# Four of eleven pairs of SwiGLU column blocks by seven products of quarters

## The chip, the cores and the metric

The kernel runs on one core of one Trainium2 chip. A core has a matrix engine (TensorE, PE in the profile; its weight loads are the row PEld), VectorE (DVE), ScalarE (ACT), GpSimd (POOL) and SyncE (SP), which run side by side and wait for each other by semaphores. Loads from device memory are issued here by SP, stores and a few small loads by POOL; an issuing engine takes its DMAs in order, and one that has to wait holds up those behind it. The metric is the device time of one launch in microseconds; lower is better.

## The reference

Two layers over 512 tokens of 1024 features, in float32. Each layer is a SwiGLU half step, a token mixer, and a second SwiGLU half step, with a layer norm after each:

```python
def swiglu(x, w13, w2):
    a, b = jnp.split(x @ w13, 2, axis=-1)
    return (jax.nn.silu(a) * b) @ w2
...
for l in range(DEPTH):
    x = layer_norm(ALPHA * x + 0.5 * swiglu(x, ffn1_w13[l], ffn1_w2[l]), ln_g[l, 0], ln_b[l, 0])
    m = mixer(x, w_in[l], ...)
    x = layer_norm(ALPHA * x + m, ln_g[l, 1], ln_b[l, 1])
    x = layer_norm(ALPHA * x + 0.5 * swiglu(x, ffn2_w13[l], ffn2_w2[l]), ln_g[l, 2], ln_b[l, 2])
```

`w13` is 1024 x 5632 (a and b of 2816 columns each), `w2` is 2816 x 1024. There are four SwiGLUs in all. The mixer is not touched by the change, except for when the transposes behind its last projection fall due.

## The kernel before

**Arithmetic.** Every float32 operand is split into a high part (ScalarE copies it to the rounded type that PE takes, line 118) and the rest (VectorE subtracts, line 119). A product is three matmuls: high times high, high times low, low times high. The features of x lie transposed in four pairs of tiles, `xh` and `xl`.

**First products of a SwiGLU (`ffn`, from line 444).** The 2816 columns of a and of b are 22 blocks of 128 columns. Block j takes a weight block of a and one of b (512 KB each, tiles `r_a`, `r_b`, loaded by SP into 4 buffers; their split parts lie in 10 buffers of the tag `w`). `proj` runs 24 matmuls 128x512 into a bank `pa` and 24 into `pb`. `glu` takes SiLU of `pa` on ScalarE and multiplies by `pb` on VectorE (line 463) into the tile `r` of the pair of blocks k and k+11. So there are eleven pairs, made in the order 8, 9, 10, 0, 1, ..., 7, with 96 matmuls each. The first pair of a SwiGLU that follows another stage runs in halves of 256 tokens, since the tokens' features come in halves.

**Sums for the second products.** The product with `w2` is done by seven products of quarters in place of eight (Winograd's form of Strassen's scheme); class `Seven` prepares and runs it. When a pair of blocks is done, `activation_sums(k)` makes four sums and two splits of `r` on VectorE and ScalarE, and `weight_sums(k)` (lines 278 to 290) loads the pair's `w2` in two tiles `ra_w` and `rb_w` (512 KB each, SP), makes four sums on VectorE, three of them in place, and POOL stores each to device memory, from where `run` loads them. `ra_w` and `rb_w` come from a tag `rs` that has two buffers in all: the next pair's loads wait until the stores of this pair's sums have been read out of them.

**Second products (`run`, lines 331 to 442).** For k = 0 to 10 it loads weights and sums, splits them and runs 18 matmuls 128x512 for each k in a first phase (products P1, P6 and P5 of two token tiles each), then two more phases. P6 of k = 2 and 3 takes the tile `t22`, that of k = 0 and 1 `t20`. `later(k)` splits the two remaining sums of `r`. `norm` does the layer norm of a token tile, stores it, and puts its transposes (`to_features`) on a list of side work (`Flow`), due 11.5 us of counted matmul time later.

**Order.** A scheduler fixes each engine's order when the program is built, by its own estimate of when each instruction could run. At run time an engine takes its instructions strictly in that order, and a VectorE instruction that waits holds up all behind it. Eight banks hold PE's results, so four blocks are in flight.

Of the kernel before, what the change touches and what calls it, by code (L numbers as in the profile page):

```python
# [79 lines left out]
def trunk(ctx: ExitStack, tc, x_in, xt_in, w13, w2, w_in, w_br, w_out, ln_g, ln_b, lb_in, hgn, sgg, sgb, sgws,  # L83
# [12 lines left out]
    def bank(name):  # L96
        return psum.tile([P, 512], F32, tag="ps", name=name)
# [89 lines left out]
    def norm(t, xt, sums, g, b, last):  # L187


        nm = small("nm")  # L190
        V.tensor_scalar(nm, sums[:, 0:1], sums[:, 1:2], -1.0 / D, op0=ALU.add, op1=ALU.mult)
        sq = wk.tile([P, D], F32, tag="rs", name="sq", bufs=2)
        ssq = small("ssq")
        S.activation(sq, xt, AF.Square, bias=nm, accum_out=ssq)
        rstd = rstd_of(ssq, 1, 1.0 / D, LN_EPS / ALPHA ** 2, "rstd")
        for qs in H:
            V.scalar_tensor_tensor(xt[:, qs], xt[:, qs], nm, g[:, qs], op0=ALU.add, op1=ALU.mult)
            V.scalar_tensor_tensor(xt[:, qs], xt[:, qs], rstd, b[:, qs], op0=ALU.mult, op1=ALU.add)
            if last:
                nc.sync.dma_start(out[0, t * P:(t + 1) * P, qs], xt[:, qs])  # L200
        if not last:
            x_at[t] = dram.tile([P, D], F32, name=f"xd{t}", tag=f"xd{t}", bufs=2)
            nc.gpsimd.dma_start(x_at[t], xt)
            ready[t] = flow.add(to_features(t, xt), LN_NS)

    LN_NS = 11500.0
    ready = [None] * NT

    def need(*ts):
        for t in ts:  # L210
            if ready[t] is not None:
                flow.finish(ready[t])
                ready[t] = None

    def out_proj(nk, lhs, w_of, c, ln, tag):

        ys = [[bank(f"y{t}{q}") for q in range(2)] for t in range(NT)]
        w = {}
# [12 lines left out]
        for k in range(nk):  # L231
            w[k] = weights(w_of(k), f"{tag}{k}")
            if k < nk - tail:
                for t in range(NT):
                    unit(k, t, (0, 1))
        g, b = ln_params(*ln)
        xs = load_rows()
        begin_features()
        for t in range(NT):
            sums = small("sums", 2)  # L240
            for q in range(2):
                for k in range(nk - tail, nk):
                    unit(k, t, (q,))
                add_to(xs[t], q, c, ys[t][q], sums)
            norm(t, xs[t], sums, g, b, False)

    def load_rows():
        xs = []
# [10 lines left out]
    class Seven:  # L259
# [11 lines left out]

        def part(self, k, a):

            if k not in self.r:
                self.r[k] = quads(f"r{k}")
            return self.r[k][:, a::2, :]

        def weight_sums(self, k):
            w = self.w_of(k)
# [51 lines left out]
        def run(self, c, ln, last):  # L331
# [103 lines left out]
            for tt in range(2):  # L435
# [5 lines left out]
                add_to(xs[t], 0, c, F[tt], sums[t])  # L441
                norm(t, xs[t], sums[t], g, b, last)

    def ffn(l, i, last=False, first_of_all=False):
        made = list(range(Seven.KEPT, NH2)) + list(range(Seven.KEPT))
        seven = Seven(lambda k: w2[l, i, k])
        js = [j for k in made for j in (k, k + NH2)]

        def blocks(j, early=False):
            return (weights(w13[l, i, j], f"a{j}", early), weights(w13[l, i, NF + j], f"b{j}", early),  # L450
                    bank(f"pa{j}"), bank(f"pb{j}"))

        def pair_of(j, args, n0, n):
            wa, wb, pa, pb = args
            proj(pa, wa, 0, from_x, KT, n0, n)
            proj(pb, wb, 0, from_x, KT, n0, n)

        def glu(j, args):
            wa, wb, pa, pb = args
            k, a = j % NH2, j // NH2  # L460
            sa = wk.tile([P, T], F32, tag="sa", name="sa", bufs=NSA)
            S.activation(sa, pa, AF.Silu)
            V.tensor_tensor(seven.part(k, a), sa.rearrange("p (h t) -> p h t", h=2),  # L463
                            pb.rearrange("p (h t) -> p h t", h=2), op=ALU.mult)
            if a:
                seven.activation_sums(k)
                seven.weight_sums(k)

        start = 0 if first_of_all else 2
        first = [blocks(j, True) for j in js[:start]]  # L470
        need(0, 1)
        for z, j in enumerate(js[:start]):
            pair_of(j, first[z], 0, 256)
        need(2, 3)
        for z, j in enumerate(js[:start]):
            pair_of(j, first[z], 256, 256)
            glu(j, first[z])
        for z, j in enumerate(js[start:]):
            if z == 0 and first_of_all:
                begin_features()  # L480
                wa = load_wx(w13[l, i, j])
                for q in range(1, 4):
                    load_xt(q)
                wb = weights(w13[l, i, NF + j], "b0")
                args = wa, wb, bank("pa0"), bank("pb0")
            else:
                args = blocks(j)
            pair_of(j, args, 0, T)
            glu(j, args)
        seven.run(0.5 / ALPHA, (l, 2 * i), last)  # L490

    def gates():
# [478 lines left out]
```

## Time and profile before

| | |
|---|---|
| time, median of 3 runs | 2124.06 us (2122.80 to 2125.29) |
| the profiled execution's own time | 2122.98 us |
| its span in the trace | 2120.1 us (2.9 us lie around it) |
| PE busy | 2097.9 us, 99% of the span, 10024 matmuls |
| VectorE busy | 1226.6 us, 58% |
| ScalarE busy | 772.2 us, 36% |
| GpSimd busy | 214.6 us, 10% |
| mean granted clock of PE | 0.998 |
| moved by DMA | 381 MB, 180 GB/s on average |

Busy time counts an engine's instructions; matmuls overlap, so what one matmul costs is read from the distance between starts, not from its own length. The chain of work is the profile's path back from the last instruction to what released it. A timeline row gives start, length, engine, line, operation, tiles, and in brackets the idle time ahead of it with what ended it. The waits list who waited for whom. A row of a DMA gives size and median time from issue to landing. Line numbers are those of the kernel before.

### The profile page before, as it was taken

To read this page: it belongs to the slowest core of one execution; us is meant where nothing else is said; L and a number is where in the kernel's file an instruction comes from. 1 tells how busy PE (TensorE), PEld (TensorE's weight loads), DVE (VectorE), ACT (ScalarE), POOL (GpSimd) and SP (SyncE) were. 2 spreads that over 40 slices of the span, in tenths; PEclk is the share of its full clock that TensorE was granted. 3 is DMA by queue.
4 is the path that set the end of the run, shared out by engine and by line. 5 is a ranking of instruction groups with operands and counts; after the bars stand their busy time and mean duration, and the time that the engine had idled before them with its cause. 6 is when DMAs were issued, how large, how long until landed. Compare 5 with 4: busy or idle time off the path is not lost.

```text
span 2120.1 us, 26533 instructions
## 1 busy us (share of the span) xinstructions
PE 2097.9 (99%) x10024; PEld 1761.5 (83%) x10024; DVE 1226.6 (58%) x2019; ACT 772.2 (36%) x1090; POOL 214.6 (10%) x360
## 2 busy tenths in 40 slices
PE   8999999999999999999999999999999999999998
PEld 6888888888888888888898888888888888888886
DVE  5545578843535644548754456779344456454586
ACT  4222455224322422226522234552333324222363
POOL 0101002001000110101111010020010001110101
PEclk9999999999999999999999999999999999999999
DMA  7665777122242465557757557761222426655674
GB/s 268 215 209 179 251 254 263 42 80 80 82 157 90 162 235 185 192 207 275 249 186 235 179 203 237 273 227 42 89 89 89 141 90 202 211 192 201 224 262 143
DMA packets 113905, 381.01 MB, mean 180 GB/s; under 512 B 14321, under 2 KB 14577, under 8 KB 113777
## 3 DMA queue, kind: packets, MB, share of 16 engines
q1 hardware_dynamic: 88848, 291.68, 42.0%
q0 software_dynamic: 24928, 87.64, 10.9%
q8 instruction: 78, 1.28, 0.2%
q14 instruction: 51, 0.41, 0.1%
HBM read 311.11 MB, written 68.16 MB: 179 GB/s over the span
## 4 chain that ended last, share of the span: by engine, by line
PE 80%; DVE 2%; ACT 1%; DMA 1%; POOL 0%; issue 0%; POOLq 0%; DVEq 0%; ACTq 0%
PE pa L143 17%; PE pb L143 16%; PE z L143 8%; PE pA L341 4%; PE pC L341 4%; PE y L143 4%; PE y L226 3%; PE pF L341 2%; PE q L143 2%; PE pE L341 2%; PE f L143 2%; PE pB L341 2%; PE i L551 2%; PE g L143 2%; PE v L551 2%; PE u L143 2%
## 5 line engine op out<-in xcount | busy, mean ns | idle before, releaser
L143 PE MATMUL pa<-xh,h_a 128*128 128x512 f32 (+1 forms) x752 | 285.0, 379 | 11.2 <-ACT xh L118 11.0
L143 PE MATMUL pa<-xl,h_a 128*128 128x512 f32 (+1 forms) x752 | 284.6, 378 | 0.1
L143 PE MATMUL pa<-xh,l_a 128*128 128x512 f32 (+1 forms) x752 | 283.7, 377 | 0.0
L143 PE MATMUL pb<-xh,h_b 128*128 128x512 f32 (+1 forms) x752 | 283.1, 377 | 0.0
L143 PE MATMUL pb<-xh,l_b 128*128 128x512 f32 (+1 forms) x752 | 282.4, 376 | 0.3 <-DVE l_b L119 0.3
L143 PE MATMUL pb<-xl,h_b 128*128 128x512 f32 (+1 forms) x752 | 282.4, 375 | 0.0
L119 DVE TENSOR_TENSOR l_b<-r_b,h_b 128x1024 fp32r<-128x1024 f32 x132 | 161.5, 1224 | 166.4 <-ACT h_b L118 165.8
L118 ACT ACTIVATE h_b<-r_b 128x1024 fp32r<-128x1024 f32 x132 | 139.9, 1060 | 303.6 <-PE pa L143 245.4
L463 DVE TENSOR_TENSOR r<-sa,pb 128x512 f32<-128x512 f32 x88 | 60.5, 688 | 303.3 <-PE pb L143 303.3
L118 ACT ACTIVATE h_a<-r_a 128x1024 fp32r<-128x1024 f32 (+1 forms) x89 | 93.5, 1051 | 278.9 <-PE pb L143 264.2
L143 PEld LDWEIGHTS pa<-xh,h_a 128*128 128x128 f32 x752 | 142.9, 190 | 38.4 <-ACT xh L118 12.6
L143 PEld LDWEIGHTS pa<-xl,h_a 128*128 128x128 f32 x752 | 142.2, 189 | 28.0 <-DVE xl L119 2.3
L143 PEld LDWEIGHTS pa<-xh,l_a 128*128 128x128 f32 x752 | 142.4, 189 | 25.6
L143 PEld LDWEIGHTS pb<-xl,h_b 128*128 128x128 f32 x752 | 141.7, 188 | 25.8
L143 PEld LDWEIGHTS pb<-xh,l_b 128*128 128x128 f32 x752 | 141.6, 188 | 26.1 <-DVE l_b L119 0.8
L143 PEld LDWEIGHTS pb<-xh,h_b 128*128 128x128 f32 x752 | 141.7, 188 | 25.5
L119 DVE TENSOR_TENSOR l_a<-r_a,h_a 128x1024 fp32r<-128x1024 f32 (+1 forms) x89 | 107.7, 1210 | 16.2 <-ACT h_a L118 12.3
L143 PE MATMUL z<-xh,h_z 128*128 128x512 f32 x256 | 102.6, 401 | 0.0
L285 POOL DMA_DIRECT2D t<-t x44 | 23.9, 543 | 763.8 <-DVE t L284 697.5
L143 PE MATMUL z<-xh,l_z 128*128 128x512 f32 x256 | 99.8, 390 | 0.0
L143 PE MATMUL z<-xl,h_z 128*128 128x512 f32 x256 | 99.8, 390 | 0.0
L119 DVE TENSOR_TENSOR l_z<-r_z,h_z 128x1024 fp32r<-128x1024 f32 x32 | 39.2, 1225 | 72.5 <-ACT h_z L118 72.4
(270 smaller groups left out, 4246.5 us busy)
## 6 DMA issues: line engine op xcount, KB each, us to landing
r_b<-in_w_dram SPq DMA_DIRECT2D x88, 512.0 KB, 4.7
r_a<-in_w_dram SPq DMA_DIRECT2D x87, 512.0 KB, 4.7
ra_w<-in_w_dram SPq DMA_DIRECT2D x44, 512.0 KB, 5.5
rb_w<-in_w_dram SPq DMA_DIRECT2D x44, 512.0 KB, 5.2
t<-ra_w POOLq DMA_DIRECT2D x88, 256.0 KB, 2.6
r_c<-in_w_dram SPq DMA_DIRECT2D x44, 512.0 KB, 6.3
r_d<-t SPq DMA_DIRECT2D x44, 512.0 KB, 4.6
r_z<-in_w_in_dram SPq DMA_DIRECT2D x32, 512.0 KB, 3.5
```

Of the source, the lines that this page charges most:

```text
L118: S.activation(hi, src, AF.Copy)
L119: V.tensor_tensor(lo, src, hi.bitcast(F32), op=ALU.subtract)
L143: PE.matmul(ps[:, n0:n0 + n], a[:, cs], m[:, n0:n0 + n], start=(i == 0), stop=(i == 3 * nk - 1))
L226: PE.matmul(ys[t][q], a[:, ts], m[:, q * 512:(q + 1) * 512], start=(k == 0 and i == 0), stop=(k == nk - 1 and i == 2))
L285: nc.gpsimd.dma_start(self.t1[k], t1)
L341: PE.matmul(ps[tt], a[:, ts], m, start=(start and k == 0 and z == 0), stop=(stop and k == NH2 - 1 and z == 2), skip_group_check=not start)
L463: V.tensor_tensor(seven.part(k, a), sa.rearrange("p (h t) -> p h t", h=2), pb.rearrange("p (h t) -> p h t", h=2), op=ALU.mult)
L551: PE.matmul(pss[t], a[k // 2][:, k % 2, ts], m[:, cs], start=(k == 0 and i == 0), stop=(k == KT - 1 and i == 2))
```

## The change

Of the eleven pairs of blocks, pairs 0 to 3 of each SwiGLU are now made by `seven_pair`: the 1024 input features and the 512 tokens are halved, a and b are the two column halves, and seven products of quarters take the place of eight. A product is 24 matmuls 128x256 for the pair's two blocks, so a pair is 168 matmuls 128x256 in place of 96 of 128x512. The sums that the scheme needs are made on VectorE: those of x once per SwiGLU (`x_sums`), those of the weights per pair (`t13`, `t2`, and `rc` in place), and the sums of the results while they are taken out of the banks. The tiles `rc` and `rd` hold two quarters of the pair's weights each; they come from the tag `rs`, the two buffers of `ra_w` and `rb_w`.

The order is now: pairs 8, 9 and 10 in the plain form, each with both kinds of sums; `weight_sums(0)`; pairs 0 to 3 by seven products, with no sums for the second products; then the plain pairs 4 to 7, each followed by the activation sums of two pairs and two `weight_sums`. The last one, pair 7's, follows the last pair as before. `norm` takes the delay of the transposes as an argument: 9.5 us in `out_proj`, 11.5 us in `run`.

```diff
+    def x_sums():
...
+        r = [slot(f"xr{q}") for q in range(4)]
+        for q in range(4):
+            V.tensor_tensor(r[q], xh[q].bitcast(F32), xl[q].bitcast(F32), op=ALU.add)
...
+            V.tensor_tensor(x3[:, 2 * q:2 * q + 2], a11, a21, op=ALU.subtract)
+            V.tensor_tensor(a21, a21, a22, op=ALU.subtract)
+            V.tensor_tensor(a22, a11, a21, op=ALU.subtract)
+            V.tensor_tensor(a12, a12, a22, op=ALU.subtract)
...
+        for c in ("s2", "s1", "s3", "s4"):
+            hi, lo = (quads(f"x{c}{v}", F32R) for v in "hl")
+            for q in range(2):
+                split(hi[:, 2 * q:2 * q + 2], lo[:, 2 * q:2 * q + 2], parts[c][q])
...
+    def seven_pair(seven, w13_of, s, k):
+        js = (k, k + NH2)
+        ra = [wk.tile([P, 2, 512], F32, tag="raw", name=f"r_p{j}", bufs=NRAW) for j in js]
+        rc, rd = (wk.tile([P, 2, 512], F32, tag="rs", name=f"r{c}{k}", bufs=2) for c in "cd")
+        t13 = [slot(f"t13{j}") for j in js]
+        t2 = slot(f"t2{k}")
+        for z, j in enumerate(js):
+            wa, wb = w13_of(j), w13_of(NF + j)
+            nc.sync.dma_start(ra[z][:, 0], wa[:, H[0]])
+            nc.sync.dma_start(ra[z][:, 1], wb[:, H[1]])
+            nc.sync.dma_start(rd[:, z], wb[:, H[0]])
+            nc.sync.dma_start(rc[:, z], wa[:, H[1]])
...
+        p = [parts(ra[z], f"p{j}") for z, j in enumerate(js)]
+        for z in range(2):
+            V.tensor_tensor(t13[z], ra[z], rd[:, z:z + 1].broadcast_to([P, 2, 512]), op=ALU.add)
+            V.tensor_tensor(t2[:, z], ra[z][:, 0], t13[z][:, 1], op=ALU.add)
+        w2 = parts(t2, f"t2{k}")
+        wt = [parts(t13[z], f"t{j}") for z, j in enumerate(js)]
+        w21 = parts(rc, f"c{k}", True)
+        V.tensor_tensor(rc, rc, t2, op=ALU.add)
+        w4 = parts(rc, f"d{k}", True)
...
+        product(A, [p[0][0], p[1][0]], "A11")
+        S.activation(upper, A, AF.Copy)
+        product(B, w2, "s2")
+        V.tensor_tensor(upper, upper, B, op=ALU.subtract)
+        product(C, [wt[0][0], wt[1][0]], "s1")
+        V.tensor_tensor(b1, C, upper, op=ALU.subtract)
+        product(E, [wt[0][1], wt[1][1]], "s3")
+        V.tensor_tensor(b1, b1, E, op=ALU.subtract)
+        product(A, w21, "A12", False)
+        S.activation(lower, A, AF.Silu)
+        product(C, [p[0][1], p[1][1]], "s4", False)
+        V.tensor_tensor(b0, C, upper, op=ALU.subtract)
+        V.tensor_tensor(lower, lower, b0, op=ALU.mult)
+        product(E, w4, "A22", False)
+        V.tensor_tensor(upper, E, upper, op=ALU.add)
+        S.activation(upper, upper, AF.Silu)
+        V.tensor_tensor(upper, upper, b1, op=ALU.mult)
...
+        seven.weight_sums(next(sums))
+        for k in by_seven:
+            seven_pair(seven, w13_of, s, k)
+        rest = by_seven + plain_last
+        for z, k in enumerate(plain_last):
+            plain(k)
+            for v in rest[2 * z:2 * z + 2]:
+                seven.activation_sums(v)
+            for _ in range(2 if z < len(plain_last) - 1 else 8):
+                v = next(sums, None)
+                if v is not None:
+                    seven.weight_sums(v)
```

**VectorE where pair 10 ends, in the first SwiGLU (the other three stand alike).** `ra_w210` and `rb_w210` hold pair 10's `w2`, `ra_w20` and `rb_w20` pair 0's; `l_a`, `l_b` are low parts of weight blocks; `rd0`, `rc0`, `t130`, `t1311`, `t20` belong to the seven products of pair 0, `l_c0` and `l_t20` are low parts of their weights. Before, from the last result of pair 10 on:

```order
L463 TENSOR_TENSOR r10_538<-sa_602,pb21_553 128x2x256
L308 TENSOR_TENSOR s12_605<-r10_538 128x256
L284 TENSOR_TENSOR t1_622<-ra_w210_620 128x512
L309 TENSOR_TENSOR s12_605<-r10_538,s12_605 128x256
L311 TENSOR_TENSOR r10_538<-r10_538 128x256
L289 TENSOR_TENSOR ra_w210_620<-rb_w210_621,ra_w210_620 128x512
L312 TENSOR_TENSOR r10_538<-r10_538,s12_605 128x256
L119 TENSOR_TENSOR tl10_607<-s12_605,th10_606 128x512
L289 TENSOR_TENSOR ra_w210_620<-ra_w210_620 128x512
L119 TENSOR_TENSOR l_a1_791<-r_a1_788,h_a1_790 128x1024
L289 TENSOR_TENSOR rb_w210_621<-rb_w210_621,ra_w210_620 128x512
L119 TENSOR_TENSOR l_b1_797<-r_b1_794,h_b1_796 128x1024
```

Now, from pair 10's last two weight sums on:

```order
L292 TENSOR_TENSOR ra_w210_661<-ra_w210_661 128x512
L292 TENSOR_TENSOR rb_w210_662<-rb_w210_662,ra_w210_661 128x512
L287 TENSOR_TENSOR t1_676<-ra_w20_674 128x512
L292 TENSOR_TENSOR ra_w20_674<-rb_w20_675,ra_w20_674 128x512
L292 TENSOR_TENSOR ra_w20_674<-ra_w20_674 128x512
L292 TENSOR_TENSOR rb_w20_675<-rb_w20_675,ra_w20_674 128x512
L493 TENSOR_TENSOR t130_691<-r_p0_687,rd0_690 128x1024
L494 TENSOR_TENSOR t20_693<-r_p0_687,t130_691 128x512
L493 TENSOR_TENSOR t1311_692<-r_p11_688,rd0_690 128x1024
L494 TENSOR_TENSOR t20_693<-r_p11_688,t1311_692 128x512
L120 TENSOR_TENSOR l_c0_727<-rc0_689,h_c0_726 128x1024
L120 TENSOR_TENSOR l_t20_715<-t20_693,h_t20_714 128x1024
```

Before, pair 10's sums are followed by the low parts of blocks that are two and more ahead, and pair 0's weight sums come a pair later. Now pair 0's weight sums follow at once, and behind them stand the sums that pair 0's second product needs.

**SP at the same place.** `r_a`, `r_b` are plain weight blocks, `r_p1` and `r_p12` quarters of pair 1. Before:

```order
L124 DMA r_a11_699<-in_w13_dram 128x1024
L124 DMA r_b11_705<-in_w13_dram 128x1024
L124 DMA r_a1_788<-in_w13_dram 128x1024
L124 DMA r_b1_794<-in_w13_dram 128x1024
L282 DMA ra_w210_620<-in_w2_dram 128x1024
L283 DMA rb_w210_621<-in_w2_dram 128x1024
L124 DMA r_a12_854<-in_w13_dram 128x1024
L124 DMA r_b12_860<-in_w13_dram 128x1024
L124 DMA r_a2_942<-in_w13_dram 128x1024
L124 DMA r_b2_948<-in_w13_dram 128x1024
L282 DMA ra_w20_775<-in_w2_dram 128x1024
L283 DMA rb_w20_776<-in_w2_dram 128x1024
```

Now:

```order
L480 DMA r_p1_920<-in_w13_dram 128x512
L481 DMA r_p1_920<-in_w13_dram 128x512
L480 DMA r_p12_921<-in_w13_dram 128x512
L481 DMA r_p12_921<-in_w13_dram 128x512
L285 DMA ra_w210_661<-in_w2_dram 128x1024
L286 DMA rb_w210_662<-in_w2_dram 128x1024
L285 DMA ra_w20_674<-in_w2_dram 128x1024
L286 DMA rb_w20_675<-in_w2_dram 128x1024
L482 DMA rd0_690<-in_w13_dram 128x512 x2
L483 DMA rc0_689<-in_w13_dram 128x512 x2
L480 DMA r_p2_1153<-in_w13_dram 128x512
L481 DMA r_p2_1153<-in_w13_dram 128x512
```

Before, four loads of weight blocks stand between two loads of `w2`. Now the loads of `w2` for pair 10, those for pair 0 and the quarters `rd0` and `rc0` follow each other directly; all three take the two buffers of the tag `rs`.

**VectorE where the first products end and `run` begins.** `r7` is the last pair's result, `ra_w27` and `rb_w27` its `w2`, `l_t22` and `l_b3` low parts that `run` needs for k = 2 and 3. Before:

```order
L463 TENSOR_TENSOR r7_1779<-sa_1843,pb18_1794 128x2x256
L308 TENSOR_TENSOR s12_1846<-r7_1779 128x256
L284 TENSOR_TENSOR t1_1858<-ra_w27_1856 128x512
L309 TENSOR_TENSOR s12_1846<-r7_1779,s12_1846 128x256
L311 TENSOR_TENSOR r7_1779<-r7_1779 128x256
L289 TENSOR_TENSOR ra_w27_1856<-rb_w27_1857,ra_w27_1856 128x512
L312 TENSOR_TENSOR r7_1779<-r7_1779,s12_1846 128x256
L119 TENSOR_TENSOR tm7_1847<-s12_1846,tm7_1847 128x512
L289 TENSOR_TENSOR ra_w27_1856<-ra_w27_1856 128x512
L119 TENSOR_TENSOR l_t22_1959<-r_t22_1956,h_t22_1958 128x1024
L289 TENSOR_TENSOR rb_w27_1857<-rb_w27_1857,ra_w27_1856 128x512
L119 TENSOR_TENSOR l_b3_1990<-r_b3_1986,h_b3_1989 128x1024
```

Now:

```order
L120 TENSOR_TENSOR tl6_2286<-s12_2284,th6_2285 128x512
L562 TENSOR_TENSOR r7_2217<-sa_2281,pb18_2232 128x2x256
L311 TENSOR_TENSOR s12_2295<-r7_2217 128x256
L287 TENSOR_TENSOR t1_2307<-ra_w27_2305 128x512
L312 TENSOR_TENSOR s12_2295<-r7_2217,s12_2295 128x256
L314 TENSOR_TENSOR r7_2217<-r7_2217 128x256
L292 TENSOR_TENSOR ra_w27_2305<-rb_w27_2306,ra_w27_2305 128x512
L315 TENSOR_TENSOR r7_2217<-r7_2217,s12_2295 128x256
L120 TENSOR_TENSOR tm7_2296<-s12_2295,tm7_2296 128x512
L292 TENSOR_TENSOR ra_w27_2305<-ra_w27_2305 128x512
L120 TENSOR_TENSOR l_t22_2408<-r_t22_2405,h_t22_2407 128x1024
L292 TENSOR_TENSOR rb_w27_2306<-rb_w27_2306,ra_w27_2305 128x512
```

The rows are the same; what differs is that the weight sums ahead of them come two to a pair, where they came one to a pair.

More of the change, by code (lines that the diff above doesn't have):

```diff
@@ L185, in add_to, with norm @@
         V.scalar_tensor_tensor(xt[:, H[q]], v, c, xt[:, H[q]], op0=ALU.mult, op1=ALU.add, **kw)
-    def norm(t, xt, sums, g, b, last):
+    def norm(t, xt, sums, g, b, last, wait=11500.0):
         nm = small("nm")
@@ L478, in ffn @@
[L478 to L486, printed above, removed]
-                args = blocks(j)
-            pair_of(j, args, 0, T)
-            glu(j, args)
+        kept = Seven.KEPT
+        plain_first = list(range(kept, NH2))
@@ new lines, in ffn, with plain @@
+        by_seven = list(range(S_PAIRS))
+        plain_last = list(range(S_PAIRS, kept))
+        sums = iter(list(range(kept, NH2)) + list(range(kept)))
+        def plain(k):
+            for j in (k, k + NH2):
+                args = blocks(j)
+                pair_of(j, args, 0, T)
+                glu(j, args)
+        k0 = plain_first[0]
+        js = (k0, k0 + NH2)
+        if first_of_all:
+            begin_features()
+            wa = load_wx(w13_of(js[0]))
+            for q in range(1, 4):
+                load_xt(q)
+            wb = weights(w13_of(NF + js[0]), "b0")
+            args = wa, wb, bank("pa0"), bank("pb0")
+            pair_of(js[0], args, 0, T)
+            glu(js[0], args)
+            args = blocks(js[1])
+            pair_of(js[1], args, 0, T)
+            glu(js[1], args)
+        else:
+            first = [blocks(j, True) for j in js]
+            need(0, 1)
+            for z, j in enumerate(js):
+                pair_of(j, first[z], 0, 256)
+            need(2, 3)
+            for z, j in enumerate(js):
+                pair_of(j, first[z], 256, 256)
+                glu(j, first[z])
@@ new lines, in ffn @@
+        seven.activation_sums(k0)
+        s = x_sums()
+        seven.weight_sums(next(sums))
+        for k in plain_first[1:]:
+            plain(k)
+            seven.activation_sums(k)
+            seven.weight_sums(next(sums))
+        seven.weight_sums(next(sums))
+        for k in by_seven:
+            seven_pair(seven, w13_of, s, k)
+        rest = by_seven + plain_last
+        for z, k in enumerate(plain_last):
+            plain(k)
+            for v in rest[2 * z:2 * z + 2]:
[4 more added lines that the diff above has]
+                    seven.weight_sums(v)
```

63 lines of the change are left out of this document (44 added, 19 removed).

## The prediction

> **What bounds the kernel now.** I read the page first, then the chain of waits in order of time, a table by stretches, and timelines of single engines. The page's head and the row of PE among its forty slices:
>
> ```profile
> span 2120.1 us, 26533 instructions
> PE 2097.9 (99%) x10024; PEld 1761.5 (83%) x10024; DVE 1226.6 (58%) x2019; ACT 772.2 (36%) x1090; POOL 214.6 (10%) x360
> PE   8999999999999999999999999999999999999998
> ```
>
> PE is the bound from end to end; what counts is how many columns PE streams, and every gap. The chain, in the second SwiGLU of the first layer and at the start of the third:
>
> ```profile
> 774.55 5.44 PE pb L143 x24
> 779.99 5.44 PE pa L143 x24
> 785.43 5.44 PE pb L143 x24
> ...
> 1060.89 2.87 PE pa L143 x24
> ```
>
> A group of 24 matmuls 128x512 takes 5.44 us, so one is worth 0.2267 us; 24 of 128x256 take 2.87 us, 0.1196 us each. Half the columns cost 53% of the time. One pair of blocks, then `run`, in the table by stretches (length, busy time of PE, PEld, DVE, ACT, POOL, clock, DMA share, GB/s):
>
> ```profile
> 779.99:801.75 21.76, 21.76 (x98) 18.02 (x97) 10.90 (x16) 6.22 (x9) 3.24 (x6) 1.00 0.68 230
> 955.00:1047.00 92.00, 92.00 (x414) 76.02 (x414) 75.09 (x101) 54.14 (x72) 10.28 (x16) 1.00 0.78 264
> ```
>
> A plain pair takes 21.76 us and VectorE is half idle in it. VectorE's groups by shape:
>
> ```profile
> L119 DVE TENSOR_TENSOR l_b<-r_b,h_b 128x1024 fp32r<-128x1024 f32 x132 | 161.5, 1224 | 166.4 <-ACT h_b L118 165.8
> L463 DVE TENSOR_TENSOR r<-sa,pb 128x512 f32<-128x512 f32 x88 | 60.5, 688 | 303.3 <-PE pb L143 303.3
> L118 ACT ACTIVATE h_b<-r_b 128x1024 fp32r<-128x1024 f32 x132 | 139.9, 1060 | 303.6 <-PE pa L143 245.4 <-PE pb L143 31.2 <-PE pC L341 14.7
> ```
>
> **Fewer columns.** A pair by seven products is 168 x 0.1196 = 20.09 us of PE in place of 96 x 0.2267 = 21.76: 1.67 less. Sixteen pairs: **-26.7 us**, with no gap. The Trainium skill ("TensorE: Matmul & The Clock Gate", section Back-to-back issue gap) gives a warm gap of N/2.4 + 2.5 ns, estimates of 109 and 216 ns; by it a pair would save 2.4 us and sixteen 38. Both spacings in this trace are 11 ns longer, so the rows decide.
>
> **VectorE inside the seven products.** A pair now needs ten operations of 1024 columns (seven splits, the two `t13`, `rc`) and nine of 512 (two for `t2`, seven on results): 10 x 1.224 + 9 x 0.688 = 18.4 us, against 20.09 of PE. Its order puts the next pair's sums between the waits on results, and I count it as hidden: the buffers of `t13` come free with the fourth product and those of `p` with the sixth, and the low parts of the next `t13` are due 8.6 us after the sixth (three products), with some 5 us of work queued ahead. Without that cover a pair would take VectorE's time (a rival below). `x_sums` is 4 x 1.224 + 16 x 0.688 = 16 us per SwiGLU; the plain pairs 8 to 10 leave VectorE 21.76 - 10.9 = 11 us each, and the low parts of two to four blocks are made ahead: nothing.
>
> **The hand-over to the seven products.** This is where I expect the loss. `ra_w`, `rb_w`, `rd` and `rc` share two buffers. Three users follow each other directly: pair 10's weight sums, pair 0's, and the quarters of pair 0; each has to be stored before the next is loaded. And pair 10's sums stand behind the result of its last block, which VectorE can only take when PE has ended the last plain block. So two round trips through device memory begin when PE runs out of plain work, and all that PE has meanwhile is the first product (2.87 us); the second needs `t2`, a sum with `rd0`. In the trace of before, the same trip is there with PE busy beside it. VectorE, POOL's stores and SP's loads around 779.99, the end of pair 10:
>
> ```profile
> 780.10 0.69 DVE L463 TENSOR_TENSOR r<-sa,pb 128x512 f32<-128x512 f32 x1 [3.42 <-PE pb L143]
> 783.98 0.69 DVE L289 TENSOR_TENSOR ra_w<-ra_w 128x512 f32<-128x512 f32 x1
> 784.58 1.22 DVE L119 TENSOR_TENSOR l_a<-r_a,h_a 128x1024 fp32r<-128x1024 f32 x1
> 785.71 0.69 DVE L289 TENSOR_TENSOR rb_w<-rb_w,ra_w 128x512 f32<-128x512 f32 x1
> ...
> 784.96 0.54 POOL L290 DMA_DIRECT2D t<-ra_w  x1
> 786.70 0.54 POOL L290 DMA_DIRECT2D t<-rb_w  x1 [1.20 <-DVE rb_w L289]
> ...
> 790.15 0.33 SPq L282 DMA_DIRECT2D ra_w<-in_w_dram  x1
> 792.66 0.33 SPq L283 DMA_DIRECT2D rb_w<-in_w_dram  x1
> ```
>
> From the end of the pair to the last store it is 6.7 us; without the split `l_a` between (1.13) 5.6. From a store to the load that takes its buffer it is 5.2 (`ra_w`) and 6.0 us (`rb_w`). Two pairs on, where POOL has no activation sums to store:
>
> ```profile
> 828.48 0.54 POOL L290 DMA_DIRECT2D t<-ra_w  x1 [1.00 <-DVE ra_w L289]
> 830.22 0.54 POOL L290 DMA_DIRECT2D t<-rb_w  x1 [1.20 <-DVE rb_w L289]
> ...
> 831.00 0.33 SPq L282 DMA_DIRECT2D ra_w<-in_w_dram  x1
> 834.07 0.33 SPq L283 DMA_DIRECT2D rb_w<-in_w_dram  x1
> ```
>
> Here it is 2.5 and 3.9 us. Landings: the `rb_w` issued at 792.66 took 5.9 us (first line below, from that tile's own answer), three `ra_w` between 715 and 800 took 2.9 to 5.2 (second), the mixer's loads on quiet queues 3.5, quarter-megabyte loads 4.2:
>
> ```profile
> DMA to landing us min/median/max: 5.9/5.9/5.9
> ...
> DMA to landing us min/median/max: 2.9/4.5/5.2
> ...
> r_z<-in_w_in_dram SPq DMA_DIRECT2D x32, 512.0 KB, 3.5
> r_b<-in_w_dram SPq DMA_DIRECT2D x44, 256.0 KB, 4.2
> ```
>
> So, from the end of pair 10: last store 5.6; `rb_w20` landed after 3.9 + 2.9 = 6.8 at the least, 6.0 + 5.9 = 11.9 at the most; queues are emptier than at 790 but the activation sums of pair 10 are stored beside it, so I take the middle, rounded up, 9.6: 15.2. Two sums and the store of the second (0.6, then 784.96 - 783.98 = 1.0): 16.9. Second trip: 2.5 + 2.9 = 5.4 to 5.2 + 5.9 = 11.1; nothing else is in flight, so 7.5, near the lower end: 24.4. Then `t130`, `t20`, `t1311`, `t20`: 3.6 us, 28.0; ScalarE's copy or VectorE's `l_c0`, 1.1, and the split `l_t20`, 1.2: 30.3. PE idles from 2.9 to there, less two matmuls that the high part lets through: **27.2 us per SwiGLU, 109 in all** (22.3 to 33.1 each, 89 to 133, by the bounds). The Trainium skill ("DMA: Bandwidth & Descriptors", section Anatomy of one DMA) counts 2.0 us + bytes/436 GB/s per DMA, estimates of 2.6 us for a store and 3.2 for half a megabyte; by it each trip is 5.8 us, the stall 21.7, and the sum 22 us lower. The trace shows such times only at its quickest (2.5 and 2.9), and 5.2 to 6.0 and 5.9 in the same place under load.
>
> **The clock behind each gap.** After the gap of 2.86 us in the second SwiGLU:
>
> ```profile
> 723.25 0.58 PE L143 MATMUL pa<-xh,h_a 128*128 128x256 f32 x1 [2.86 <-ACT xh L118]
> ...
> 725.34 0.41 PE L143 MATMUL pa<-xh,l_a 128*128 128x256 f32 x1
> 725.55 0.41 PE L143 MATMUL pa<-xh,h_a 128*128 128x256 f32 x1
> ...
> 727.02 0.28 PE L143 MATMUL pa<-xl,h_a 128*128 128x256 f32 x1
> 727.14 0.28 PE L143 MATMUL pa<-xh,l_a 128*128 128x256 f32 x1
> ```
>
> For some 3.2 us starts lie 0.21 us apart, then 0.12: half speed, 15 matmuls, 1.4 us. Four stalls: **+6 us**.
>
> **Weight sums two to a pair at the end.** In pairs 4 to 7 a weight sum has 10.9 us (half a pair). Its chain: store to load 4.5 (between 3.9 and 6.0), landing 5.2 (2.9 to 5.9; `run`'s stretch has a DMA share of 0.78, so nearer the loaded row), two sums and the last store 2.3: 12.0 (9.1 to 14.2). Over the six periods from pair 1's to pair 7's it falls behind by 6 x 1.1 = 7 us. Splits are made ahead, so PE doesn't notice until `run`, where `l_t22` stands behind pair 7's sums on VectorE: with the first store 26 us into pair 4, pair 7's `rb_w` lands at 26 + 5 x 12 + 9.7 = 96 us, `l_t22` ends near 100, and PE wants it 87.0 + 2 x 4.08 + 1.4 = 96.6 us in (18 matmuls for each k). I take 4 us per SwiGLU, between 0 and 10: **+16 us**. What waits there on VectorE is all of `run`'s splits.
>
> **Transposes.** Due 2 us earlier in the two `out_proj`; if the norm isn't ready PE waits up to those 2 us, if it is, nothing changes: I take 0, -1 to +4 in all.
>
> **The sum**, against the profiled execution's own 2122.98 us (1.1 below the median): 2122.98 - 26.7 + 109 + 6 + 16 = **2227 us**. By the bounds alone, -26.7 + 89 + 6 - 1 and -26.7 + 133 + 6 + 40 + 4, it is 2190 to 2279; the terms won't all be at one end, so 2193 to 2265.
>
> **Rivals.** *Short trips* (0.15): with SP and POOL idle but for this chain, every store and load runs at the quickest row: trips of 6.8 and 5.4 us, 4.9 less per stall, 2227 - 20 = 2207, and 2191 without the end's wait. For it: the DMA share of 0.68 falls to almost nothing. Against: even the mixer's quiet loads took 3.5. *VectorE paces the seven products* (0.12): 18.4 of 20.1 us leaves 1.7 us a pair, and every wait on a result that comes late eats into it. If a pair takes 22 us, the gain turns to a loss of 0.2 and the sum is 16 x 1.9 = 30 us more: 2257. Against: while a result is late VectorE has the next pair's sums. *The hand-over is hidden* (0.04), the case on the other side: pair 10's and pair 0's weight sums run while PE still has plain work, and only the 26.7 us remain: 2096 us. It decides where the hand-over and the clock together cost under 6.7 us per SwiGLU, that is if the quarters land within 6 us of pair 10's end. Against: pair 10's sums stand behind its last result on a strict queue. *The change gives PE no less work* (0.03): if matmuls of 256 columns cost 0.130 us with 168 weight loads in a row, a pair by seven products takes 21.8 us; 2254. Against: the 24 at 1060.89 also load weights for each matmul.
>
> **Chances.** The forecast 0.65, the rivals 0.15, 0.12, 0.04, 0.03, and 0.01 for an even result. A change of under 0.2% (4 us) can't be told from none here. Faster 0.04, same 0.01, slower 0.95. For 8 in 10 the range takes the forecast's own span, short trips and most of the VectorE case: 2187 to 2268.
>
> **What would show it.** Right: four gaps of PE of 22 to 33 us, each behind the first product of pair 0 (24 matmuls 128x256), with VectorE idle before `t130` on a DMA and SP waiting for POOL's stores; seven products of 2.87 us in a row otherwise; a short gap at k = 2 of `run`. Wrong: PE without a gap there; matmuls of 256 columns further apart than 0.12 us in pairs 1 to 3; gaps inside these pairs behind VectorE; or weight sums of pair 10 ahead of its last result.

## The result and the profile after

The changed kernel takes 2224.45 us (median of 4 runs, 2219.12 to 2229.12), the kernel before, beside it on the same chip, 2124.68 us (4 runs, 2122.80 to 2125.55). The ratio is 1.0473, 95% interval 1.0454 to 1.0492: slower by some 100 us. The profiled execution took 2219.12 us, the shortest of the four, with a span of 2217.4 us, 97.3 more than before. The comparisons below are with that span.

The head of the page after, PE's row and that of its clock among the forty slices:

```profile
span 2217.4 us, 29219 instructions
PE 2091.0 (94%) x11176; PEld 1808.6 (82%) x11176; DVE 1457.3 (66%) x2307; ACT 845.2 (38%) x1186; POOL 212.0 (10%) x360
...
PE   8599999999999959999995999999999999599998
...
PEclk9799999999999979999997999999999999799999
```

PE does 6.9 us less in all and fills 94% of the span instead of 99%. Four slices have a 5 where all was 9, and the clock dips to 7 in the same four. They are the four hand-overs to the seven products. PE's waits after (who waited for whom: sum, times, longest):

```profile
PE fB L516 <- ACT h_t L119: 93.2, 4, 23.5
PE pB L344 <- DVE l_t L120: 14.4, 4, 5.0
PE pa L144 <- ACT xh L119: 6.3, 2, 5.4
```

The first row is the hand-over, the second k = 2 of `run`, both at the places that were named. The third is the wait for transposed features; the kernel before has 11.0 us there:

```profile
PE pa L143 <- ACT xh L118: 11.0, 3, 5.6
```

The first hand-over on PE: first and last matmul of product 1, first of product 2 (`fB`), the end of the slow clock, and the last matmul of pair 3:

```profile
76.00 0.28 PE L516 MATMUL fA<-xh,h_p 128*128 128x256 f32 x1
...
78.75 0.28 PE L516 MATMUL fA<-xh,l_p 128*128 128x256 f32 x1
102.15 0.58 PE L516 MATMUL fB<-xs2h,h_t 128*128 128x256 f32 x1 [23.12 <-ACT h_t L119]
...
107.83 0.38 PE L516 MATMUL fB<-xs2h,h_t 128*128 128x256 f32 x1
108.04 0.29 PE L516 MATMUL fB<-xs2l,h_t 128*128 128x256 f32 x1
108.17 0.29 PE L516 MATMUL fB<-xs2h,l_t 128*128 128x256 f32 x1
...
182.92 0.28 PE L516 MATMUL fE<-xh,l_d 128*128 128x256 f32 x1
```

Behind the gap starts lie 0.21 us apart, from 108.04 on 0.12. From 76.00 to 182.92 it is 106.92 us. Twenty-eight products of 24 x 0.12 = 2.88 us, less the one spacing behind the last start, would be 80.5. So the hand-over costs 26.4 us, gap and slow clock together. The other three, read in the same way, cost 27.0, 26.1 and 26.3: **105.8 us** in all.

What PE waits for, in the same stretch, on VectorE, POOL and SP in order of time:

```profile
76.27 0.69 DVE L562 TENSOR_TENSOR r<-sa,pb 128x512 f32<-128x512 f32 x1 [9.28 <-PE pb L144]
...
81.85 0.54 POOL L293 DMA_DIRECT2D t<-rb_w  x1 [0.19 <-issue]
...
85.29 0.33 SPq L286 DMA_DIRECT2D rb_w<-in_w_dram  x1
88.72 0.69 DVE L287 TENSOR_TENSOR t<-ra_w 128x512 f32<-128x512 f32 x1 [7.17 <-DMA ra_w<-in_w_dram]
90.06 0.69 DVE L292 TENSOR_TENSOR ra_w<-rb_w,ra_w 128x512 f32<-128x512 f32 x1 [0.65 <-DMA rb_w<-in_w_dram]
...
91.77 0.54 POOL L293 DMA_DIRECT2D t<-ra_w  x1 [0.19 <-issue]
92.50 0.54 POOL L293 DMA_DIRECT2D t<-rb_w  x1 [0.19 <-issue]
94.37 0.80 SPq L482 DMA_DIRECT2D rd<-in_w_dram  x2
...
97.15 1.23 DVE L493 TENSOR_TENSOR t<-r_p,rd 128x1024 f32<-128x1024 f32 x1 [4.95 <-DMA rd<-in_w_dram]
...
102.33 1.22 DVE L120 TENSOR_TENSOR l_t<-t,h_t 128x1024 fp32r<-128x1024 f32 x1
```

Two trips stand one behind the other. Pair 10's last result is taken at 76.27 and the last store of its sums is issued at 81.85; the second half of pair 0's `w2` is loaded from 85.29 on and used at 90.06; the last two stores of its sums are issued at 91.77 and 92.50, the first quarters from 94.37 on, and they are used at 97.15. Meanwhile VectorE has nothing to do for 7.17 and 4.95 us.

### The profile page after: what moved, and what is told of

Read it like the earlier page. It is cut to its first block, busy times and chain, and to the rows that moved or that the text cites. A ratio compares the mean times of both kernels' runs of the same rounds, so it can differ in the third digit from the quotient of the medians.

```text
span 2217.4 us, 29219 instructions
## 1 busy us (share of the span) xinstructions
PE 2091.0 (94%) x11176; PEld 1808.6 (82%) x11176; DVE 1457.3 (66%) x2307; ACT 845.2 (38%) x1186; POOL 212.0 (10%) x360
## 5 line engine op out<-in xcount | busy, mean ns | idle before, releaser
L144 PE MATMUL pa<-xh,h_a 128*128 128x512 f32 (+1 forms) x496 | 184.5, 372 | 6.3 <-ACT xh L119 6.3
L144 PE MATMUL pa<-xl,h_a 128*128 128x512 f32 (+1 forms) x496 | 184.9, 373 | 0.1
L144 PE MATMUL pa<-xh,l_a 128*128 128x512 f32 (+1 forms) x496 | 183.6, 370 | 0.0
L144 PE MATMUL pb<-xh,h_b 128*128 128x512 f32 (+1 forms) x496 | 183.2, 369 | 0.0
L144 PE MATMUL pb<-xh,l_b 128*128 128x512 f32 (+1 forms) x496 | 182.9, 369 | 0.3 <-DVE l_b L120 0.3
L144 PE MATMUL pb<-xl,h_b 128*128 128x512 f32 (+1 forms) x496 | 182.8, 368 | 0.0
L516 PE MATMUL fB<-xs2h,h_t 128*128 128x256 f32 x128 | 40.8, 319 | 93.2 <-ACT h_t L119 93.2
L144 PEld LDWEIGHTS pa<-xh,h_a 128*128 128x128 f32 x496 | 94.0, 190 | 23.0 <-ACT xh L119 7.5
L144 PEld LDWEIGHTS pa<-xl,h_a 128*128 128x128 f32 x496 | 93.9, 189 | 18.0 <-DVE xl L120 2.5
L144 PEld LDWEIGHTS pa<-xh,l_a 128*128 128x128 f32 x496 | 94.0, 189 | 15.5
L144 PEld LDWEIGHTS pb<-xh,h_b 128*128 128x128 f32 x496 | 93.4, 188 | 15.5
```

The source lines that it names most:

```text
L144: PE.matmul(ps[:, n0:n0 + n], a[:, cs], m[:, n0:n0 + n], start=(i == 0), stop=(i == 3 * nk - 1))
L516: PE.matmul(ps[:, half[z]], a[:, ms], v, start=start, stop=(m == 3 and i == 2), skip_group_check=not (first and z == 0))
```

## The experiments

The table gives for each kernel the median, the time that pairs 0 to 3 take beyond 80.5 us (first matmul of pair 0 to last of pair 3, sum over the four SwiGLUs) and what the first products of `run` take beyond the kernel before (first matmul into `pA` to first into `pE`, 74.94 us there, sum over four). These two columns are differences of starts in PE's timeline of the one profiled execution, the median is that of all.

| kernel | median, us | pairs 0 to 3, us over | `run`, us over |
|---|---|---|---|
| the change | 2224.45 | 105.8 | 23.0 |
| e1: own tiles | 2142.33 | 20.0 | 22.0 |
| e2: sums ahead | 2206.95 | 85.7 | 30.0 |
| e3: one trip | 2213.62 | 66.3 | 58.0 |
| e4: transposes | 2230.08 | 106.1 | 26.5 |
| e5: own tiles, four buffers | 2102.87 | 16.5 | 0.1 |
| e6: e5, pair 0's sums later | 2093.02 | 3.9 | 0.4 |
| e7: e5, a sum in each pair | 2118.82 | 30.9 | 0.4 |
| e8: four shared buffers | 2165.58 | 77.1 | 0.0 |
| e9: e6 with five pairs | 2142.92 | 4.3 (five pairs, beyond 100.7) | 56.7 |

The kernel before had medians of 2124.73 beside e1 to e4, 2121.07 beside e5 to e7 and 2123.24 beside e8 and e9.

### e1: tiles of their own for the quarters

```diff
-        rc, rd = (wk.tile([P, 2, 512], F32, tag="rs", name=f"r{c}{k}", bufs=2) for c in "cd")
+        rc, rd = (slot(f"r{c}{k}") for c in "cd")
```

> The quarters rc and rd get tiles of their own from the big pool instead of the two buffers of the weight sums; nothing else is edited. Shared-buffer theory (the gaps at the hand-over are the wait of the quarters for the stores of the sums of pairs 10 and 0): the four gaps of 23 us and the slow clock behind them go, the 5 us gaps at k = 2 of run stay: about 2120 us (2110 to 2130). Rival, strict queue (the gap comes from VectorE taking pair 10's last result and its sums before any work for the seven products, whatever the buffers): a gap of 6 us or more remains at each hand-over, 2145 us or more. Rival, VectorE paces the seven products: pair 0's sums now fall among them and lengthen pairs 0 and 1 by up to 2.8 us per SwiGLU, 2131 us.

Measured: 2142.33 us (5 runs, 2131.70 to 2152.01), ratio 1.0085 (1.0054 to 1.0115). In the profile, of an execution of 2131.70 us, the row of 93.2 us is gone:

```profile
PE pB L344 <- DVE l_t L120: 14.9, 4, 4.9
PE fC L516 <- DVE b L529: 14.2, 4, 6.2
```

With its own buffers `t130` also runs ahead of pair 10's last result on VectorE: it starts at 71.73, the result is taken at 80.08. So this one edit takes away both halves of the mechanism, the trip and the place behind the result; e2, e3 and e8 take them apart. What is new is a gap of 1.8 to 6.2 us later in pair 0, before the second product into bank C. The first of them on PE, then VectorE ahead of it:

```profile
94.57 0.58 PE L516 MATMUL fC<-xs4h,h_p 128*128 128x256 f32 x1 [3.58 <-DVE b L529]
```

```profile
86.70 0.68 DVE L292 TENSOR_TENSOR rb_w<-rb_w,ra_w 128x512 f32<-128x512 f32 x1
87.31 0.68 DVE L527 TENSOR_TENSOR r<-r,fB 128x512 f32<-128x512 f32 x1
...
93.22 0.69 DVE L287 TENSOR_TENSOR t<-ra_w 128x512 f32<-128x512 f32 x1
93.83 0.68 DVE L529 TENSOR_TENSOR b<-fC,r 128x512 f32<-128x512 f32 x1
```

None of these rows has an idle time: VectorE works through, with two pairs' sums of `w2` beside the seven products, and takes bank C too late. That is the rival "VectorE paces" at one place, the pair behind the hand-over. The shared-buffer theory holds for the 93.2 us; the time is 22 us above what it gave, mostly for these gaps and the slow clock behind them, and above its range (2110 to 2130).

### e10: the same kernel once more

> The kernel of the first experiment once more, unchanged, since its times lay between 2131.7 and 2152.0 us and the profile was of the shortest. If what varies is when the quarters of pair 0 land (their loads stand in SP's queue behind pair 10's sums), a longer execution has gaps before the second or third product of pair 0 that the first profile lacked, of the size of the difference. If it is the end, the gaps at k = 2 of run are longer than 14.9 us in all.

Measured: 2142.20 us (a single execution, on another chip than e1's), span 2140.4, 10.6 more than in the first profile. Pairs 0 to 3 take 7.2 us more in all and the first products of `run` 3.9. `t130` of the first SwiGLU waits longer for its quarter (first the first profile, then this one):

```profile
71.73 1.23 DVE L493 TENSOR_TENSOR t<-r_p,rd 128x1024 f32<-128x1024 f32 x1 [5.51 <-DMA rd<-in_w_dram]
```

```profile
74.16 1.22 DVE L493 TENSOR_TENSOR t<-r_p,rd 128x1024 f32<-128x1024 f32 x1 [7.81 <-DMA rd<-in_w_dram]
```

The wait is longer in all four SwiGLUs, by 2.3, 0.8, 2.1 and 0.4 us, and pairs 0 to 3 take 3.1, 0.6, 3.0 and 0.6 us more in the same order. So between these two executions 7.2 us come with a later landing of the quarters, which has almost no slack in this kernel, and 3.9 from the end. That the other executions scatter for the same reason is not shown.

### e2: the same buffers, the sums ahead of the last plain pairs

```diff
-        for k in plain_first[1:]:
+        for z, k in enumerate(plain_first[1:]):
+            for _ in range(1 + z):
+                seven.weight_sums(next(sums))
             plain(k)
             seven.activation_sums(k)
-            seven.weight_sums(next(sums))
-        seven.weight_sums(next(sums))
```

> The buffers stay shared; in the program the weight sums of pair 9 are put ahead of pair 9, those of pairs 10 and 0 ahead of pair 10, so that they no longer stand behind pair 10's last result. Shared-buffer theory with the strict queue behind the last result: the two trips run beside plain work; what is left behind the last result are its product, the activation sums and the sums of the quarters on VectorE, some 9 us less the 2.9 us of the first product: gaps of about 6 us instead of 23, about 2150 us (2135 to 2170). If the gap came from the loads of the quarters being slow by themselves, it would stay above 14 us: 2185 us or more.

Measured: 2206.95 us (4 runs), ratio 1.0392 (1.0376 to 1.0407): a miss by 57 us. The gaps are 17.4 to 20.4 us. SP's loads for the sums and of the first quarters, then the first use of the quarters and the gap:

```profile
50.44 0.33 SPq L285 DMA_DIRECT2D ra_w<-in_w_dram  x1
...
65.39 0.33 SPq L285 DMA_DIRECT2D ra_w<-in_w_dram  x1
...
76.89 0.33 SPq L285 DMA_DIRECT2D ra_w<-in_w_dram  x1
...
87.17 0.80 SPq L482 DMA_DIRECT2D rd<-in_w_dram  x2
```

```profile
90.60 1.23 DVE L493 TENSOR_TENSOR t<-r_p,rd 128x1024 f32<-128x1024 f32 x1 [2.52 <-DMA rd<-in_w_dram]
97.23 0.58 PE L516 MATMUL fB<-xs2h,h_t 128*128 128x256 f32 x1 [18.05 <-ACT h_t L119]
```

No weight sum stands behind the last result now, yet the quarters are issued 11 us after PE has run out of plain work (76.1 here). The sums of pairs 9, 10 and 0 take the two buffers in turn, one pair every 10 to 15 us, and the first load is issued only at 50.44, since pair 8's sums had the buffers until then. I had counted the trips as hidden without adding them up: three from 50.44 on end at 87, and the plain work at 76. The strict queue behind the last result is only one way to be late; the other is the rate at which two buffers turn over. The time and the gaps are those that I had set down for the other theory, loads of the quarters that are slow by themselves; but the quarters issued at 87.17 are used at 90.60, 3.4 us later. They are issued late, not slow.

### e3: one trip instead of two

```diff
-        seven.weight_sums(next(sums))
         for k in by_seven:
             seven_pair(seven, w13_of, s, k)
```

> The weight sums of pair 0 are taken out of the hand-over, all later ones move up by one place, so that the last pair is followed by two sums. Shared-buffer theory: one trip instead of two at the hand-over, gaps of about 14 us instead of 23 (37 us less in all); one more sum in the chain at the end, which is already behind, so the gaps at k = 2 of run grow from 5 to 14 to 17 us (40 to 48 more): 2228 us (2215 to 2240). If the end's gap were not set by the chain of weight sums, it would stay at 5 us: 2188 us.

Measured: 2213.62 us (4 runs, 2206.03 to 2218.53), ratio 1.0418 (1.0387 to 1.0448).

```profile
PE fB L516 <- ACT h_t L119: 55.1, 4, 13.9
PE pB L344 <- DVE l_t L120: 16.9, 4, 6.1
PE pA L344 <- ACT h_b L119: 14.8, 4, 4.4
PE pA L344 <- DVE l_b L120: 8.5, 5, 2.3
```

The hand-over's gaps are 13.7 to 13.9 us, as expected: the second trip was worth 9.5 us per SwiGLU. The sum that was moved comes back at the end: the gaps of `run` grow from 14.4 us to 40.2 in all, by 6.5 per SwiGLU where 9 to 12 were expected, and the time lies 1.4 us below its range; with the slow clock, `run` loses 8.8 more per SwiGLU (58.0 against 23.0 in the table). The end is set by the chain of weight sums.

### e8: four buffers, still shared

```diff
-    NS, NRAW, NSA = 33, 4, 3
+    NS, NRAW, NSA = 31, 4, 3
```

and `bufs=4` in place of 2 at every tile of the tag `rs`.

> The quarters stay in the tag of the weight sums, but the tag has four buffers (two slots fewer in the big pool); order as in the change. Pair 0's sums now load ahead into the other two buffers, and only the quarters wait for the stores of pair 10's sums: one trip behind pair 10's last result. If each trip behind that result is worth what the experiment with one trip showed, the gaps are about 14 us at each hand-over (56 us in all), and the end has none: about 2165 us (2150 to 2178). If it were the number of buffers and not what stands behind the last result, the gaps would be under 5 us: 2115 us or less.

Measured: 2165.58 us (4 runs, 2164.66 to 2165.86), ratio 1.0199 (1.0182 to 1.0216).

```profile
PE fB L516 <- ACT h_t L119: 64.9, 4, 16.9
```

One trip is left, and with it a gap of 16 us; the end has none. In e3, also with one trip, the gap is 13.8: there the first quarters are used 3.1 us after their issue, here 4.6, while the stores of pair 0's sums go out beside them. So the number of buffers does not cure the hand-over. A quarter that takes over a buffer of pair 10's sums is late, with two or with four, because these sums stand behind the last result. It does cure the end.

### e5 and e6: own tiles and four buffers, then pair 0's sums behind the seven products

e5 joins the edits of e1 and e8, e6 adds that of e3.

> The quarters have tiles of their own as in the first experiment, and the tag of the weight sums has four buffers instead of two, with two slots fewer in the big pool to pay for them. What is left in the trace of the first experiment: 14.9 us of gaps at k = 2 of run, 14.2 us before the second product into bank C of pair 0, and some 6 us of slow clock behind each kind. Chain theory for the end (with two buffers the store and the next load stand in line, some 11 us for each pair's sums; with four they overlap): the end's gaps go, about 2112 us in the profiled execution (2105 to 2120). Rival for the end, VectorE's load (pairs 4 to 7 have 22 us each and VectorE about as much work): the gaps stay, 2131 us. The gaps of pair 0 stay in both.

> As the kernel with four buffers, and the weight sums of pair 0 stand behind the seven products instead of ahead of them, so that the last pair is followed by two sums. If the gaps in pair 0 come from VectorE, which has the sums of two pairs of w2 beside the seven products there, they shrink to under 1 us per SwiGLU; the one sum more at the end costs under 4 us per SwiGLU with four buffers: 2095 us (2088 to 2112). If pair 0's gaps come from late loads of the quarters, they stay, and the time is that of the kernel with four buffers or more.

Measured: e5 2102.87 us (4 runs), ratio 0.9917 (0.9902 to 0.9932); e6 2093.02 us (4 runs, 2091.29 to 2095.64), ratio 0.9872 (0.9857 to 0.9887). PE's waits, e5 first, then e6:

```profile
PE fB L516 <- DVE l_t L120: 6.3, 5, 1.4
PE pa L144 <- ACT xh L119: 5.4, 1, 5.4
PE fC L516 <- DVE b L529: 4.0, 3, 1.6
PE fB L516 <- ACT h_t L119: 1.9, 1, 1.9
```

```profile
PE pa L144 <- ACT xh L119: 5.7, 2, 5.4
PE fB L516 <- DVE l_t L120: 1.4, 4, 0.8
PE fC L516 <- DVE b L529: 0.8, 3, 0.3
```

e5 came out below its range (2105 to 2120). I had left the gaps of pair 0 as they were, but with four buffers VectorE makes pair 0's sums right behind pair 10's and takes bank C before it turns to pair 1, where in e1 work for pair 1 came first; the wait before C falls from 14.2 to 4.0 us. The end's gaps are gone with four buffers, so they were the chain of trips and not VectorE's load. In e6 pairs 0 to 3 take 80.5 to 82.5 us per SwiGLU: the seven products run within 2 us of the 80.5 that the arithmetic gives. It beats both kernels, by 28 us the one before. PE's work accounts for 4 x (4 x 21.76 - 4 x 20.16) = 25.6 of that.

### e7: weight sums inside the seven products

e5 with `seven.weight_sums(next(sums))` behind each `seven_pair`.

> As the kernel with four buffers, with one pair's weight sums behind each pair by seven products: VectorE gets four operations of 512 columns more in each, 2.8 us, which makes 21.2 us against the 20.16 us that the seven products take on PE in the trace. VectorE-paces theory: pairs 0 to 3 take 21 us or more each, 4 to 8 us more per SwiGLU than without, and the end has no gap: 2115 to 2140 us. Rival (what VectorE lacks in a pair it has ahead): the products stay 2.88 us apart in pairs 1 to 3, 2100 us.

Measured: 2118.82 us (10 runs, 2116.52 to 2123.45), ratio 0.999 (0.998 to 1.000), 16 us over e5, from which it differs by these sums alone, and 26 over e6. Pairs 0 to 3 take 14.4 us more than in e5, 3.6 per SwiGLU. One of the two longest gaps:

```profile
1855.32 0.58 PE L516 MATMUL fB<-xs2h,h_t 128*128 128x256 f32 x1 [2.32 <-ACT h_t L119]
```

VectorE has no idle time in the 19 us ahead of this gap: it does pace when it gets 2.8 us more per pair, and with what e5 loses in pair 0 that undoes nearly the whole gain. It isn't spread over all pairs, as I had it: most of it falls on pairs 0 and 1, and most products of pairs 2 and 3 are 2.88 us apart. The largest loss there, 2.8 us in pair 2 of the third SwiGLU, comes behind quarters for which VectorE waits 2.36 us, so not all of it is VectorE's load.

### e9: five pairs instead of four

e6 with `S_PAIRS = 5` and the later sums three to a pair.

> The kernel with tiles of its own, four buffers and the sums of pair 0 behind the seven products, with five pairs by seven products instead of four, the later sums three to a pair. PE has 4 x 1.6 = 6.4 us less. VectorE has, by 18.4 us a pair by seven products, 10.9 a plain one, 5.7 for the sums of each pair and 16 for x, 236 us in the first products of a SwiGLU, PE 231. VectorE-paces theory: it falls behind by 5 us and more per SwiGLU, and the time is 2100 to 2125 us. Rival (VectorE has room in run to catch up): 2087 us.

Measured: 2142.92 us (4 runs), ratio 1.0090 (1.0075 to 1.0105), 50 us over e6 and 18 over the upper end of what I expected.

```profile
PE pB L344 <- DVE l_t L120: 33.6, 4, 9.5
```

The loss isn't where the theory put it: the five pairs take about 1 us over per SwiGLU, and the first products of `run` take 56.7 us over in all. The sums that the seven products put off don't fit into three plain pairs. VectorE isn't full there: in the first SwiGLU, from the end of the seven products to 12 us into `run`, it idles for 24 of 77 us. Between 239 and 262 it waits 7.2 us in all for loads of `ra_w` and `rb_w`, just ahead of the gap of 9.5 us at 263.2. So the trips have a part in it; what the order on VectorE adds is open.

### e4: the delay of the transposes

```diff
-            norm(t, xs[t], sums, g, b, False, 9500.0)
+            norm(t, xs[t], sums, g, b, False)
```

> Only the delay of the transposes in the two out_proj goes back from 9.5 to 11.5 us. The prediction had 0 for this edit (minus 1 to plus 4). The trace has 6.3 us of waits for transposed features after the change where it had 11.0 before: if the delay is the cause, this kernel is some 5 us slower than the changed one, 2229 us; if it is chance, 2224 us.

Measured: 2230.08 us (4 runs, 2224.66 to 2231.80), 5.6 over the change.

```profile
PE pa L144 <- ACT xh L119: 10.9, 4, 5.4
```

The waits are back at 10.9 us, as in the kernel before (11.0). The ten traces with the shorter delay have 5.4 to 7.2 us in this row, the two with the longer one 10.9 and 11.0, so the delay takes some 5 us of waits away. The times agree with that but would not show it alone: the ranges of the two kernels overlap.

## Why the prediction was right, and where it was off

The forecast was 2227 us, the median is 2224.45. The direction, the place and the cause were right: slower, by two trips through shared buffers while PE has one product of work. One trip less (e3) makes each gap 9.5 us shorter, and buffers of their own (e1) end it. The changes of span by the terms, from the traces of before and after:

| term | forecast | measured | from |
|---|---|---|---|
| fewer columns | -26.7 | -25.6 | 28 products of 2.88 us per SwiGLU against four pairs of 21.76 |
| hand-over and the clock behind it | +109 and +6 | +105.8 | timeline of PE, four SwiGLUs |
| the end, with its clock | +16 | +23.0 | first products of `run` |
| transposes | 0 | -4.7 | waits for `xh`, 11.0 to 6.3 |
| sum | +104 | +98.5 | the span grew by 97.3 |

That 2227 lies so near the median is partly luck. The gaps were forecast 16 us too dear in all (109, measured 93.2) and the transposes 5; the clock behind the gaps was 7 too cheap (6, measured 12.6) and the end 7. None of these errors is large enough to touch the direction.

**Fewer columns: right.** Products in pairs 1 to 3 are 2.88 us apart, and e6 shows the gain on the clock of the whole kernel. The Trainium skill's warm gap ("TensorE: Matmul & The Clock Gate", section Back-to-back issue gap), by which I had an alternative of -38, is not borne out for these matmuls, each of which loads its own weights: starts lie 0.12 us apart, not 0.109.

**The hand-over: right in kind, 9 us too dear in all, gap and clock together.** From pair 10's end at 76.0 to the last store of pair 0's sums it was 16.5 us, 16.9 by the forecast, though by two errors that cancel: the trip from 81.85 to 90.06 took 8.2 us and not 9.6, the sums and stores around it 1 us more. It was the second trip that I mis-sized. I took 7.5 us from the last store, but `rd` takes `ra_w`'s buffer, and its store goes out 0.7 us earlier; with a load of 2.8 us the quarter was there 4.65 us after the last store. From there to PE it took 5.0 us and not 5.7. The rival "short trips" (6.8 and 5.4) was half right for the first trip and right for the second, 5.4 us from the store at 91.77. The gap came out at 23.3 us, much nearer to its 22.3 than to the forecast's 27.2: on the length of the gap the rival was the better one.

**The clock: too cheap.** I took 1.4 us behind each stall from the one short gap in the trace of before. Less the gap, the hand-overs lose 12.6 us, 3.1 each, in which some short waits for `h_t` and `l_t` lie too.

**The end: right in place, too cheap.** The chain of sums falls behind and shows at `pB` of k = 2. In the first SwiGLU `l_t22` is ready 101.9 us after the start of pair 4, where I had 100, and PE wants it at 97.0, where I had 96.6:

```profile
285.02 0.79 PE L344 MATMUL pB<-l_t,th 128*128 128x512 f32 x1 [5.00 <-DVE l_t L120]
```

The gaps are 2.1 to 5.0 us, 14.4 in all, near the 16; the other 8.6 us are lesser waits and the slow clock behind them, which I had not counted at this place.

**Transposes: wrong.** I took 0, with a wait if the norm was not ready and no change if it was. But in the trace of before PE waits for transposed features behind `out_proj` twice, 2.86 and 2.58 us; with the transposes due earlier these two waits went, and 4.7 us with them in all (e4).

**VectorE inside the seven products: right in the count, by luck for the change.** The 18.4 us of VectorE do fit under the seven products: in e6, with no stall to rest in and with pair 10's sums beside them, the four pairs stay within 2 us of the arithmetic. What the term left out is that VectorE then also has pair 0's sums. In the change it does both pairs' sums during the hand-over, while PE stands still, so the pairs behind it start with nothing owed. As soon as the hand-over is hidden (e1), both pairs' sums fall into pair 0, and 20 us come back there. The stall had hidden this cost. The rival "VectorE paces" was thus the next bound, not a rival.

## What to carry to other kernels

Tiles that share a tag share a queue: before a new user is put into an old tag, list who used the buffers last, what these users wait for, and how much work the bound engine has in that time. Adding up the turns of a buffer pair (10 to 15 us each here) is worth more than judging each one as hidden. And when a stall is removed, look again at every engine that rested in it: its slack may have been the stall.

## What the runs showed of the hardware that was not expected

The length of a gap alone doesn't say what it costs in clock. In the trace after, behind the first hand-over (length, busy times of PE, PEld, DVE, ACT and POOL, granted clock, DMA share, GB/s):

```profile
102.15:105.15 3.00, 2.84 (x10) 2.33 (x11) 3.00 (x4) 1.84 (x2) 0.00 (x0) 0.50 0.96 346
105.15:108.15 3.00, 3.00 (x16) 3.00 (x16) 1.88 (x3) 1.06 (x1) 0.00 (x0) 0.52 0.07 20
108.15:111.15 3.00, 3.00 (x27) 3.00 (x26) 2.79 (x3) 1.54 (x2) 0.00 (x0) 1.00 0.26 76
```

Half speed lasts 5.9 us here, 4.8 to 6.7 behind the other three gaps of 23 us, where the gap of 2.86 us in the kernel before had 3.2. A longer gap did not cost more: behind the gaps of 13.7 to 13.9 us in e3 it lasted 3.8 to 6.2. Behind the six gaps of 1.4 to 1.6 us in e5 the granted clock does not fall, and one matmul starts 0.22 us ahead of the next instead of 0.12. The four gaps of 2.3 us in e7, all at the same place, are followed by half speed for 3.41, 3.41, 0 and 6.83 us.

The records of the granted clock show a pattern. Within each trace its switches all lie on one grid of 3.41 us, so every stretch at half speed is a whole number of such steps long: one step in the kernel before, two at three gaps of `run` in the kernel after, seven, eight, seven and seven at its four hand-overs (23.9 or 27.3 us, most of it while PE stands still). The grid does not start anew with a gap: in e7 the clock falls 0.6 us after one gap of 2.3 us has ended and 2.3 us after another. That the cost of a short gap hangs on where it falls on this grid would fit these figures; no experiment moved a gap along it. The Trainium skill ("TensorE: Matmul & The Clock Gate", section Part 1: The HAM clock gate) gives some 3.4 us of work until full speed; that is one step of the grid, and the stretches here reach from under that to twice as much.
